# A two-block recurrent and attention model on one core: the values' product per head on its half of the array, sums through DRAM as whole rows, and eight planned times

## The chip, the cores and the metric

The kernel runs on one core of a Trainium2 chip. The metric is the device time of one execution in microseconds (us). Five engines work from queues of their own: TensorE (PE; PEld is its weight load), VectorE (DVE), ScalarE (ACT), GpSimd (POOL) and SyncE (SP), which here issues nearly all transfers. Each engine takes its instructions in the order in which the program has them, so an instruction that waits holds back all that stand behind it on the same engine.

## The reference, cut to what matters

Two blocks of two layers each, over 512 positions of width 1024. Each layer of the first block has three branches (a recurrence with a state per head, a retention, a gated unit), a gated merge of them, and a feed-forward part. The change touches the recurrence and two normalisations:

```python
def step(state, inp):                      # rwkv7_scan, per head of 64
    r_t, w_t, k_t, v_t, kk_t, a_t = inp
    sa = jnp.einsum('bhvk,bhk->bhv', state, -kk_t)
    state = (state * w_t[:, :, None, :] + sa[..., None] * (kk_t * a_t)[:, :, None, :]
             + v_t[..., None] * k_t[:, :, None, :])
    y = jnp.einsum('bhvk,bhk->bhv', state, r_t)
    return state, y
...
kk = kk / jnp.maximum(jnp.sqrt(jnp.sum(kk * kk, axis=-1, keepdims=True)), 1e-12)
y = rwkv7_scan(r, decay, k, v, kk, a)
mean = jnp.mean(y, axis=-1, keepdims=True)
var = jnp.mean(jnp.square(y - mean), axis=-1, keepdims=True)
y = (y - mean) * lax.rsqrt(var + RW_GN_EPS) * lnx_g + lnx_b
y = y + jnp.sum(r * k * r_k, axis=-1, keepdims=True) * v
...
y = y * lax.rsqrt(jnp.mean(y * y, axis=-1, keepdims=True) + EPS)     # retention, per head of 128
```

## The kernel before, in words

Activations lie with features on the 128 partitions and the 512 positions along the row. Every dense product is made of three matmuls of 128x512 (lines 170 to 172, tiles `pm`, and `pbr` in the merge) on weights that stream in by 512 KB and are split by ACT (`whi`, line 161) and DVE (`wlo`, line 162). A dense tile of the first block is 24 such matmuls; a product of the merge is 12. Two banks of TensorE's result memory serve `pm` and `pbr` in turn, so a tile can't start before the one two places ahead of it has been read out (`gate`, line 428; in the merge line 940, on DVE).

The recurrence of a layer works on four pairs of heads (f = 0 to 3) and four chunks each. `rw_pair` prepares a pair, two lanes of `rw_unit` compute the 16 units (pair and chunk), and `rw_final` chains the chunks' states, normalises the outputs `y` and multiplies by the gate. In a unit, `psy` takes for each of the two heads e one product with `uw` (line 685) and one with the values (line 686). The values `vp` stand in a tile of 128x4x64 with zeros in the two middle columns, so that each head's weights are 128 columns wide, half of them zero.

`sums` makes a sum over each head's features for every position: four small matmuls (line 202, result of 32 partitions for each quarter of the positions), a step on ACT or DVE (`fn`), a write to DRAM (`sumd`, line 207), and n reads (line 209) that spread each row over 128/n partitions again; n is 2 for the recurrence and 1 for retention. It is used 40 times: in each of the two layers four times each for `psk` (the length of kk, read by `kkr`, line 527), `psbon`, `psmean` (read at line 742), `psq` (line 755) and `psrn` of retention (line 825).

The order of TensorE's work in these layers is made by hand: `Plan` keeps a time, in which each step has a cost, and lets dense steps (`Dense`, `MORE`) fill what lies between the steps of chains. `Chain(cost, wait)` says that the thread's next step is due `wait` us later. The dense work is the projections, the other branches and then the gates (`gates1`), which run out last; behind them the merge begins. The other engines' orders come from a scheduler that follows this one. Instructions under `self.late()` are put behind the last read of a dense tile.

Of the kernel before, what the change touches and what calls it, by code (L numbers as in the profile page):

```python
# [10 lines left out]
F32 = mybir.dt.float32  # L11
# [7 lines left out]
S = 512  # L19
# [36 lines left out]
def Chain(cost, wait):  # L56
    return Step(cost, wait, chain=True)
# [49 lines left out]
class Kern:  # L107
# [90 lines left out]
    def sums(self, x, sel, n, ps, out, fn):  # L198

        nc = self.nc  # L200
        for g in range(4):
            nc.tensor.matmul(ps[32 * g:32 * g + 32, :], lhsT=sel, rhs=x[:, g * 128:(g + 1) * 128],
                             start=True, stop=True, skip_group_check=True)
        t = self.ap.tile([128, 128], F32, name="sums", tag="sums", bufs=2)
        fn(t, ps)
        d = self.dp.tile([4, 32, 128], F32, name="sumd", tag="sumd", bufs=8)
        nc.sync.dma_start(d.rearrange("g r t -> (g r) t"), t)
        for i in range(n):
            nc.sync.dma_start(out[i * 128 // n:(i + 1) * 128 // n, :].rearrange("p (g t) -> p g t", g=4),
                              d[:, i][None].to_broadcast([128 // n, 4, 128]))  # L210

# [258 lines left out]
    def rw_pair(self, l, f, r, k, vt, m, lora, half):  # L470
# [51 lines left out]
        nc.vector.scalar_tensor_tensor(r, r, v(V_RK + f), k2, op0=OP.mult, op1=OP.mult)  # L522
        yield Chain(0.4, 13.0)

# [73 lines left out]
    def lane(self, l, i):  # L598

        while self.units:  # L600
            f, g = self.units[0]
            if f > 1 and not self.ended[f - 2]:
                yield Chain(0.0, 1.0)
                continue
            self.units.pop(0)
            if g == 0:
                self.states[f] = dict((n, self.tile("WK", (128, 8, 64), name=n)) for n in ("y0", "rdw", "xt", "cc"))
            yield from self.rw_unit(f, g, self.states[f], i)
            self.left[f] -= 1
            if not self.left[f]:  # L610
                self.plan.add(self.rw_final(l, f, self.states[f]), 0, 2.0)

    def rw_unit(self, f, g, st, lane):
# [16 lines left out]
        nc.vector.tensor_copy(tk, pst[:, 1:3, :])  # L630
        vp = self.vp[lane]
        nc.scalar.activation(vp[:, 0:4:3, :], pst[:, 3, :].rearrange("p (e v) -> p e v", e=2), AF.Copy)
        rhs = small([128, 2, 128], "rhs")
# [25 lines left out]
        for e in range(2):  # L659
            nc.tensor.matmul(psv[:, e, :], lhsT=ams[e][:, 256:384], rhs=vp[:, 3 * e, :],  # L660
                             start=True, stop=True)
# [22 lines left out]
        for e in range(2):  # L684
            nc.tensor.matmul(psy[:, e, :], lhsT=uw[:, e, :], rhs=ams[e][:, 128:256], start=True, stop=False)
            nc.tensor.matmul(psy[:, e, :], lhsT=vp[:, 2 * e:2 * e + 2, :].rearrange("p a v -> p (a v)"),
                             rhs=ams[e][:, 384:512], start=False, stop=True)
        for e in range(2):
# [6 lines left out]
        for m in range(3):  # L695
            for e in range(2):
                for c in range(2):
                    cs = slice(64 * c, 64 * c + 64)
                    os = ws = slice(64 - 64 * e, 128 - 64 * e)
                    us = slice(64 * e, 64 * e + 64)  # L700
                    b_ = tk[cs, 0, us]
                    o, x, y, first, last = ((0, uw[cs, e, ws], b_, True, True), (1, b_, uw[cs, e, us], True, False),
                                            (1, tk[cs, 1, us], vp[cs, 3 * e, :], False, True))[m]
                    nc.tensor.matmul(psx[c][os, o, :], lhsT=x, rhs=y, start=first, stop=last, skip_group_check=True)
# [5 lines left out]
    def rw_final(self, l, f, st):  # L710
# [5 lines left out]
        nc.vector.tensor_tensor(cc[:, 0:7, :], cc[:, 0:7, :], d[:, 0:7].unsqueeze(2).to_broadcast([128, 7, 64]), op=OP.mult)  # L716
        yield Chain(0.0, 1.0)
        for c in range(1, 7):
# [8 lines left out]
        for c in range(1, 8):  # L727
            cs = slice(64 * c, 64 * c + 64)
            for e in range(2):
# [9 lines left out]
                  lambda t, ps: nc.scalar.activation(t, ps, AF.Copy, scale=-1.0 / 64))  # L739
        yield Chain(0.4, 10.0)  # L740
        with self.late():
# [10 lines left out]
        nc.scalar.activation(gt, psg, AF.Copy)  # L752
        yield Chain(1.6, 11.0)
        with self.late():
# [14 lines left out]
    def retention(self, l, win):  # L769
# [4 lines left out]
        for f in range(2):  # L774
# [19 lines left out]
            for e in range(2):  # L794
# [24 lines left out]
                self.norms(sq, self.sel[:, 1], 1, self.PF([128, 128], "psrn"), bias=self.eps[:, 0:1], scale=1.0 / 128)  # L819
                self.plan.add(self.ret_end(l, h, y, sq), 0, 12.0)  # L820
                yield Dense(0.4)
# [978 lines left out]
    def run(self):  # L1800
# [3 lines left out]
        with ExitStack() as ctx:  # L1804
# [11 lines left out]
            if L1:  # L1816
                g12 = self.cp.tile([128, 8], F32, name="g12")
                nc.vector.tensor_tensor(g12, V[:, 16:24], V[:, 24:32], op=OP.mult)
                with block(self, "act"):
# [13 lines left out]
                    self.am = [self.ap.tile([128, 2, 4, 128], F32, name="am%d" % i) for i in range(2)]  # L1833
                    self.vp = [self.ap.tile([128, 4, 64], F32, name="vp%d" % i) for i in range(2)]
                    for t in self.am:
                        nc.gpsimd.memset(t.rearrange("p e m t -> p (e m t)"), 0.0)
                    for t in self.vp:
                        nc.gpsimd.memset(t.rearrange("p a v -> p (a v)"), 0.0)
                    for l in range(L1):
# [303 lines left out]
```

## Time and profile before

| | |
|---|---|
| median of 3 runs | 3266.28 us (3265.93 to 3267.68) |
| profiled execution: its own time | 3264.7 us |
| profiled execution: span of the trace | 3263.0 us |
| PE busy | 3208.0 us, 98% of the span |
| DVE busy | 2187.2 us, 67% |
| ACT busy | 1362.0 us, 42% |
| mean granted clock of TensorE | 0.996 of full speed |

All times below are from the one profiled execution, counted from the start of its span. The merges of the first block's two layers begin near 487 and 1440 us. A wait is the idle time of an engine in front of an instruction, named by what ended it.

### The profile page before, as it was taken

To read this page: it belongs to the slowest core of one execution; us is meant where nothing else is said; L and a number is where in the kernel's file an instruction comes from. 1 tells how busy PE (TensorE), PEld (TensorE's weight loads), DVE (VectorE), ACT (ScalarE), POOL (GpSimd) and SP (SyncE) were. 2 spreads that over 40 slices of the span, in tenths; PEclk is the share of its full clock that TensorE was granted. 3 is DMA by queue.
4 is the path that set the end of the run, shared out by engine and by line. 5 is a ranking of instruction groups with operands and counts; after the bars stand their busy time and mean duration, and the time that the engine had idled before them with its cause. 6 is when DMAs were issued, how large, how long until landed. Compare 5 with 4: busy or idle time off the path is not lost.

```text
span 3263.0 us, 47497 instructions
## 1 busy us (share of the span) xinstructions
PE 3208.0 (98%) x17992; PEld 2574.7 (79%) x17992; DVE 2187.2 (67%) x4071; ACT 1362.0 (42%) x2442; POOL 124.9 (4%) x176
## 2 busy tenths in 40 slices
PE   8999999999999999999999999999999999999998
PEld 6787877888887787878888887877788888777777
DVE  6875656777537855656677456987666669866665
ACT  5533434444335333434444334344334443443343
POOL 0000000000000000000000000010003100100031
PEclk9999999999999999999999999999999999999999
DMA  4433245433433423245333436453355564534464
GB/s 148 132 99 88 85 137 178 127 102 97 139 107 108 130 82 96 81 156 180 101 97 98 150 122 206 143 148 109 118 194 187 175 174 139 152 109 124 151 213 145
DMA packets 199797, 434.75 MB, mean 133 GB/s; under 512 B 29833, under 2 KB 58633, under 8 KB 199569
## 3 DMA queue, kind: packets, MB, share of 16 engines
q1 hardware_dynamic: 197904, 429.62, 42.8%
q8 instruction: 142, 2.33, 0.3%
q0 software_dynamic: 512, 1.05, 0.1%
q10 hardware_dynamic: 1152, 1.05, 0.1%
q14 instruction: 87, 0.70, 0.1%
HBM read 339.05 MB, written 61.36 MB: 123 GB/s over the span
## 4 chain that ended last, share of the span: by engine, by line
PE 82%; DVE 8%; DMA 6%; issue 2%; ACT 2%; SPq 0%; POOL 0%; DVEq 0%; ACTq 0%; POOLq 0%
PE pm L170 21%; PE pm L172 21%; PE pm L171 21%; PE psy L1186 2%; PE pbr L170 2%; PE pbr L171 2%; PE pbr L172 2%; PE pspt L1176 2%; DVE wlo L162 2%; DMA rdw<-sumd 1%; DMA sqr<-sumd 1%; PE psl L1158 1%; PE psl L1159 1%; DMA sqk<-sumd 1%; DMA sumd<-sums 1%
## 5 line engine op out<-in xcount | busy, mean ns | idle before, releaser
L170 PE MATMUL pm<-shi,whi 128*128 128x512 f32 x3064 | 1227.0, 400 | 0.9 <-ACT whi L161 0.9
L172 PE MATMUL pm<-shi,wlo 128*128 128x512 f32 x3064 | 1202.2, 392 | 1.4 <-DVE wlo L162 1.4
L171 PE MATMUL pm<-slo,whi 128*128 128x512 f32 x3064 | 1201.0, 392 | 0.0
L161 ACT ACTIVATE whi<-wraw 128x1024 fp32r<-128x1024 f32 x480 | 508.4, 1059 | 887.0 <-PE pm L171 527.6
L162 DVE TENSOR_TENSOR wlo<-wraw,whi 128x1024 fp32r<-128x1024 f32 x480 | 588.1, 1225 | 198.4 <-ACT whi L161 193.1
L170 PEld LDWEIGHTS pm<-shi,whi 128*128 128x128 f32 x3064 | 577.3, 188 | 138.4 <-issue 26.9
L172 PEld LDWEIGHTS pm<-shi,wlo 128*128 128x128 f32 x3064 | 576.6, 188 | 125.8 <-DVE wlo L162 4.0
L171 PEld LDWEIGHTS pm<-slo,whi 128*128 128x128 f32 x3064 | 577.5, 188 | 111.7 <-issue 4.1
L428 DVE TENSOR_TENSOR ev<-pm,rb 128x512 f32<-128x512 f32 x138 | 94.7, 687 | 110.9 <-PE pm L172 110.1
L897 DVE TENSOR_TENSOR gate<-pm,rb 128x512 f32<-128x512 f32 x80 | 55.0, 688 | 127.3 <-PE pm L172 127.0
L170 PE MATMUL pbr<-shi,whi 128*128 128x512 f32 x288 | 113.8, 395 | 1.1 <-DVE gate L940 0.8
L170 PE MATMUL pm<-whi,shi 128*128 128x256 f32 x384 | 112.5, 293 | 1.3 <-DVE ev L428 1.3
L171 PE MATMUL pbr<-slo,whi 128*128 128x512 f32 x288 | 112.2, 390 | 0.0
L172 PE MATMUL pbr<-shi,wlo 128*128 128x512 f32 x288 | 112.2, 389 | 0.0
L171 PE MATMUL pm<-wlo,shi 128*128 128x256 f32 x384 | 108.9, 284 | 0.6 <-DVE wlo L162 0.6
L172 PE MATMUL pm<-whi,slo 128*128 128x256 f32 x384 | 108.9, 284 | 0.0
L940 DVE SCALAR_TENSOR_TENSOR gate<-gate,pbr 128x512 f32<-128x512 f32 x128 | 85.7, 683 | 29.1 <-PE pbr L172 28.5
L944 POOL TENSOR_TENSOR gate<-gate 128x512 f32<-128x512 f32 x48 | 78.0, 1626 | 590.5 <-DVE gate L940 335.6
L937 ACT ACTIVATE gate<-gate 128x512 f32<-128x512 f32 x128 | 76.2, 625 | 46.0 <-DMA gate<-gtd 40.1
L1143 ACT ACTIVATE p<-psl,st 128x256 f32<-128x256 f32 (+3 forms) x128 | 65.1, 512 | 60.4 <-DVE st L1141 50.9
L170 PEld LDWEIGHTS pm<-whi,shi 128*128 128x128 f32 x384 | 73.6, 192 | 3.8 <-DVE ev L428 1.7
L171 PEld LDWEIGHTS pm<-wlo,shi 128*128 128x128 f32 x384 | 73.8, 192 | 1.3 <-DVE wlo L162 1.1
(524 smaller groups left out, 4401.8 us busy)
## 6 DMA issues: line engine op xcount, KB each, us to landing
wraw<-in_w_gt SPq DMA_DIRECT2D x148, 512.0 KB, 3.6
wraw<-in_w_in SPq DMA_DIRECT2D x116, 512.0 KB, 3.6
wraw<-in_f_up SPq DMA_DIRECT2D x88, 512.0 KB, 3.5
gtd<-gate SPq DMA_DIRECT2D x116, 256.0 KB, 2.0
gate<-gtd SPq DMA_DIRECT2D x116, 256.0 KB, 4.2
wraw<-in_w_br SPq DMA_DIRECT2D x44, 512.0 KB, 3.7
wraw<-in_f_dn SPq DMA_DIRECT2D x44, 512.0 KB, 3.5
wraw<-in_w_out SPq DMA_DIRECT2D x32, 512.0 KB, 3.7
```

Of the source, the lines that this page charges most:

```text
L161: nc.scalar.activation(hi[:, :n], raw[:, :n], AF.Copy)
L162: nc.vector.tensor_tensor(lo[:, :n], raw[:, :n], hi[:, :n].bitcast(F32), op=OP.subtract)
L170: nc.tensor.matmul(ps, lhsT=lhs[0], rhs=rhs[0], start=first, stop=False, skip_group_check=skip)
L171: nc.tensor.matmul(ps, lhsT=lhs[0], rhs=rhs[1], start=False, stop=False, skip_group_check=skip)
L172: nc.tensor.matmul(ps, lhsT=lhs[1], rhs=rhs[0], start=False, stop=last, skip_group_check=skip)
L428: self.last = self.nc.vector.tensor_tensor(t, ps, self.rb, op=OP.mult)
L937: nc.scalar.activation(g, g, AF.Tanh, scale=0.5)
L940: nc.vector.scalar_tensor_tensor(g, g, 1.0, pb, op0=OP.add, op1=OP.mult)
L944: (nc.gpsimd if self.pre and n in self.cfg.get("pa", (1, 2, 3)) else nc.vector).tensor_tensor(g, g, acc[c], op=OP.add)
L1143: nc.scalar.activation(p[:, :w], l, AF.Exp, bias=st[:, 0:1], accum_out=st[:, 1:2])
L1176: nc.tensor.transpose(pt_[:, b * 128:(b + 1) * 128], ps[e][:, b * 128:(b + 1) * 128], self.ident)
L1186: nc.tensor.matmul(psy[64 * e:64 * e + 64, :], lhsT=vs[e][b], rhs=pts[e][:, b * 128:(b + 1) * 128], start=first and b == 0, stop=last and ...
```

## The change

In a unit, the product with the values loses its padding: `vp` becomes a tile of 128x2x64 of the unit's own, each head's weights are 64 columns, and its result goes to the head's 64 partitions alone. The order of the four products changes from uw, values, uw, values to both uw, then both values. The two padded tiles and the zeroing of them on POOL go. In `sums`, only the rows that are read later go to DRAM, n writes of four partitions instead of one of 128; a sum's 512 positions then lie in one piece, and each read fetches rows of 2 KB instead of four pieces of 512 B. Eight planned times change.

```diff
@@ sums
-        d = self.dp.tile([4, 32, 128], F32, name="sumd", tag="sumd", bufs=8)
-        nc.sync.dma_start(d.rearrange("g r t -> (g r) t"), t)
+        d = self.dp.tile([n, 4, 128], F32, name="sumd", tag="sumd%d" % n, bufs=8)
         for i in range(n):
-            nc.sync.dma_start(out[i * 128 // n:(i + 1) * 128 // n, :].rearrange("p (g t) -> p g t", g=4),
-                              d[:, i][None].to_broadcast([128 // n, 4, 128]))
+            nc.sync.dma_start(d[i], t[i:128:32, :])
+        for i in range(n):
+            nc.sync.dma_start(out[i * 128 // n:(i + 1) * 128 // n, :],
+                              d[i].rearrange("g t -> (g t)")[None].to_broadcast([128 // n, S]))
@@ rw_pair, between the sum psk and its use in kkr
-        yield Chain(0.4, 13.0)
+        yield Chain(0.4, 15.0)
@@ lane, start of rw_final; rw_final, before the chain of states
-                self.plan.add(self.rw_final(l, f, self.states[f]), 0, 2.0)
+                self.plan.add(self.rw_final(l, f, self.states[f]), 0, 2.5)
-        yield Chain(0.0, 1.0)
+        yield Chain(0.0, 2.5)
@@ rw_unit
-        vp = self.vp[lane]
-        nc.scalar.activation(vp[:, 0:4:3, :], pst[:, 3, :].rearrange("p (e v) -> p e v", e=2), AF.Copy)
+        vp = small([128, 2, 64], "vp")
+        nc.scalar.activation(vp, pst[:, 3, :].rearrange("p (e v) -> p e v", e=2), AF.Copy)
...
         for e in range(2):
-            nc.tensor.matmul(psy[:, e, :], lhsT=uw[:, e, :], rhs=ams[e][:, 128:256], start=True, stop=False)
-            nc.tensor.matmul(psy[:, e, :], lhsT=vp[:, 2 * e:2 * e + 2, :].rearrange("p a v -> p (a v)"),
-                             rhs=ams[e][:, 384:512], start=False, stop=True)
+            nc.tensor.matmul(psy[:, e, :], lhsT=uw[:, e, :], rhs=ams[e][:, 128:256], start=e == 0, stop=False,
+                             skip_group_check=True)
+        for e in range(2):
+            nc.tensor.matmul(psy[64 * e:64 * e + 64, e, :], lhsT=vp[:, e, :], rhs=ams[e][:, 384:512], start=False,
+                             stop=True, skip_group_check=True)
@@ rw_final, from psmean to its use, and from psq to its use
-        yield Chain(0.4, 10.0)
+        yield Chain(0.4, 7.5)
-        yield Chain(1.6, 11.0)
+        yield Chain(1.6, 8.5)
@@ retention, from psrn to its use
-                self.plan.add(self.ret_end(l, h, y, sq), 0, 12.0)
+                self.plan.add(self.ret_end(l, h, y, sq), 0, 9.0)
@@ run
-                    self.vp = [self.ap.tile([128, 4, 64], F32, name="vp%d" % i) for i in range(2)]
-                    for t in self.vp:
-                        nc.gpsimd.memset(t.rearrange("p a v -> p (a v)"), 0.0)
```

What this does to the orders is shown at three places. The first is TensorE in a unit of the recurrence, before:

```order
L678 MATMUL psu<-rhs,tt 128x128 x2
L685 MATMUL psy<-am_235,uw 128x128
L686 MATMUL psy<-am_235,vp_237 128x128
L685 MATMUL psy<-am_235,uw 128x128
L686 MATMUL psy<-am_235,vp_237 128x128
L704 MATMUL psx<-tk,uw 64x64 x4
```

And the same unit in the changed program:

```order
L680 MATMUL psu<-rhs,tt 128x128 x2
L687 MATMUL psy<-am_235,uw 128x128 x2
L690 MATMUL psy<-am_235,vp 64x128 x2
L708 MATMUL psx<-tk,uw 64x64 x4
L708 MATMUL psx<-uw,tk 64x64 x4
```

The two products with the values stand together, have 64 result partitions each, and stand directly ahead of the 64x64 products.

The second place is DVE around the beginning of the merge in layer 0, where `y_3695` is the output of the last pair (f = 3), line 216 the last step of its sum `psq`, line 755 its first use, and line 940 reads out a product of the merge. Before:

```order
L216 RECIPROCAL sums<-sums 128x128
L940 SCALAR_TENSOR_TENSOR gate<-gate,pbr 128x512 x2
L944 TENSOR_TENSOR gate<-gate 128x512
L162 TENSOR_TENSOR wlo<-wraw,whi 128x1024
L755 TENSOR_TENSOR y_3695<-y_3695,rdw 128x512
L940 SCALAR_TENSOR_TENSOR gate<-gate,pbr 128x512
L756 TENSOR_SCALAR y_3695<-y_3695,vec_243 128x512
```

The same place in the changed program (lines 218, 759 and 944 are those called 216, 755 and 940 above; `y_3680` is the same output):

```order
L218 RECIPROCAL sums<-sums 128x128
L430 TENSOR_TENSOR gate<-pm,rb 128x512
L162 TENSOR_TENSOR wlo<-wraw,whi 128x1024
L759 TENSOR_TENSOR y_3680<-y_3680,rdw 128x512
L944 SCALAR_TENSOR_TENSOR gate<-gate,pbr 128x512
L760 TENSOR_SCALAR y_3680<-y_3680,vec_239 128x512
L761 TENSOR_TENSOR y_3680<-y_3680,xt 128x512
L762 TENSOR_TENSOR y_3680<-cc,y_3680 128x512
L944 SCALAR_TENSOR_TENSOR gate<-gate,pbr 128x512
```

One more dense tile is read out between the sum and its use, and the use stands ahead of the merge's first read-out instead of its third. On TensorE, the four matmuls of `psq` and the one of `psgate` now stand ahead of the last 24 dense matmuls; before, the merge's first product followed on them at once. Layer 1 has the same two orders at its merge.

The third place is SP's queue there, before (line 907 stores a gate, line 934 loads one):

```order
L157 DMA wraw<-in_w_br 128x1024
L207 DMA sumd<-sums 128x128
L209 DMA rdw<-sumd 64x4x128 x2
L934 DMA gate<-gtd 128x512
L157 DMA wraw<-in_w_br 128x1024
```

And in the changed program:

```order
L157 DMA wraw<-in_w_br 128x1024
L209 DMA sumd<-sums 4x128 x2
L211 DMA rdw<-sumd 64x512 x2
L911 DMA gtd<-gate 128x512
L157 DMA wraw<-in_w_br 128x1024 x2
L938 DMA gate<-gtd 128x512 x2
```

Two small writes stand for one, and the reads have rows of 512 elements. In `rw_pair`, 60 dense matmuls stand between the matmuls of `psk` and of `psbon` (which is where `kkr` is due) for every pair in the changed program; before it was 60 for the first pair and 54 for the other three. From `psbon` on to `psA` it stays 24 for the first three pairs and becomes 30 for the fourth. (A matmul of 256 columns is counted as half of one.)

## Rows read from the trace of the kernel before

**Rows 1.** The page, busy time of TensorE and its granted clock in 40 slices.
```profile
PE 3208.0 (98%) x17992; PEld 2574.7 (79%) x17992; DVE 2187.2 (67%) x4071; ACT 1362.0 (42%) x2442; POOL 124.9 (4%) x176
PEclk9999999999999999999999999999999999999999
```

**Rows 2.** The waits of TensorE: us in total, times, longest.
```profile
PE pbr L170 <- DVE gate L940: 6.6, 4, 2.9
PE psA L546 <- DVE kkr L533: 5.6, 5, 1.8
PE psam L651 <- ACT rhs L635: 3.6, 4, 1.2
PE psu L678 <- DVE rhs L674: 1.8, 2, 1.5
```

**Rows 3.** Timeline at layer 0's merge: start, us, engine, line, [idle before].
```profile
485.82 0.43 PE L202 MATMUL psq<-rdw,sel 128*32 128x128 f32 x8
...
492.10 1.24 SPq L209 DMA_DIRECT2D rdw<-sumd  x2
...
497.61 0.39 PE L171 MATMUL pbr<-slo,whi 128*128 128x512 f32 x1
497.83 0.39 PE L172 MATMUL pbr<-shi,wlo 128*128 128x512 f32 x1
499.69 0.69 DVE L755 TENSOR_TENSOR y<-y,rdw 128x512 f32<-128x512 f32 x1 [4.33 <-DMA rdw<-sumd]
501.13 0.63 PE L170 MATMUL pbr<-shl,whi 128*128 128x512 f32 x1 [2.91 <-DVE gate L940]
```

**Rows 4.** Stretches: PE busy (instructions), PEld, DVE, ACT, POOL, granted clock, DMA share.
```profile
74.00:77.00 3.00, 2.32 (x38) 2.03 (x39) 3.00 (x5) 1.81 (x5) 0.00 (x0) 1.00 0.22 60
501.00:504.00 3.00, 2.87 (x7) 2.33 (x8) 2.90 (x5) 2.71 (x4) 0.00 (x0) 0.55 0.00 0
1027.00:1030.00 3.00, 3.00 (x8) 2.31 (x8) 2.93 (x7) 2.91 (x8) 0.00 (x0) 0.50 0.46 95
```

**Rows 5.** Timeline at layer 1's merge, TensorE.
```profile
1453.55 0.71 PE L170 MATMUL pbr<-shl,whi 128*128 128x512 f32 x1 [2.89 <-DVE gate L940]
```

**Rows 6.** Timeline of kkr on DVE and psA on TensorE, first pairs of both layers.
```profile
68.36 0.75 DVE L527 SCALAR_TENSOR_TENSOR kkr<-mix,vec,sqk 128x512 f32<-128x512 f32 x1 [1.07 <-DMA sqk<-sumd]
...
74.68 0.98 PE L546 MATMUL psA<-kr,kkr 64*64 64x64 f32 x32 [1.50 <-DVE kkr L533]
...
1019.26 0.75 DVE L527 SCALAR_TENSOR_TENSOR kkr<-mix,vec,sqk 128x512 f32<-128x512 f32 x1 [1.35 <-DMA sqk<-sumd]
...
1025.59 0.97 PE L546 MATMUL psA<-kr,kkr 64*64 64x64 f32 x32 [1.79 <-DVE kkr L533]
```

**Rows 7.** DMA issues: count, KB each, median us from issue to landing.
```profile
hi<-hi SPq DMA_DIRECT2D x68, 128.0 KB, 2.6
...
sumd<-sums SPq DMA_DIRECT2D x40, 64.0 KB, 1.8
...
sqr<-sumd SPq DMA_DIRECT2D x8, 256.0 KB, 8.3
...
rdw<-sumd SPq DMA_DIRECT2D x16, 128.0 KB, 5.7
...
cumb<-cumd SPq DMA_DIRECT2D x8, 256.0 KB, 3.7
```

**Rows 8.** Timeline of TensorE in a unit, and a pair of half-array products in block 2.
```profile
203.95 0.39 PE L685 MATMUL psy<-am,uw 128*128 128x128 f32 x2
...
204.40 0.39 PE L685 MATMUL psy<-am,uw 128*128 128x128 f32 x2
...
204.94 0.35 PE L704 MATMUL psx<-tk,uw 64*64 64x64 f32 x8
...
2785.03 0.44 PE L1186 MATMUL psy<-pt,vf 128*64 128x128 f32 x4
...
2785.40 0.50 PE L171 MATMUL pm<-slo,whi 128*128 128x512 f32 x1
```

More of the change, by code (lines that the diff above doesn't have):

```diff
@@ L659, in rw_unit @@
         for e in range(2):
-            nc.tensor.matmul(psv[:, e, :], lhsT=ams[e][:, 256:384], rhs=vp[:, 3 * e, :],
+            nc.tensor.matmul(psv[:, e, :], lhsT=ams[e][:, 256:384], rhs=vp[:, e, :],
                              start=True, stop=True)
@@ L702, in rw_unit @@
                     o, x, y, first, last = ((0, uw[cs, e, ws], b_, True, True), (1, b_, uw[cs, e, us], True, False),
-                                            (1, tk[cs, 1, us], vp[cs, 3 * e, :], False, True))[m]
+                                            (1, tk[cs, 1, us], vp[cs, e, :], False, True))[m]
                     nc.tensor.matmul(psx[c][os, o, :], lhsT=x, rhs=y, start=first, stop=last, skip_group_check=True)
```

## The prediction, before the changed kernel had run

> **What bounds the kernel now.** The page comes first. TensorE is busy for 98% of the span [rows 1], so a transfer or a step of another engine counts only where TensorE stands still for it, or slows down. The list of TensorE's waits tells where: in the first block, 6.6 us at `pbr` for the read-out on line 940 and 5.6 us at `psA` for `kkr`; next come 3.6 us at `psam` and 1.8 us at `psu`, which wait for small steps of the lanes [rows 2]. The first two are this change's subject, since both go back to `sums`.
>
> The timeline at layer 0's merge shows how. `psq` runs at 485.82; its spreading reads are issued at 492.10; DVE stands 4.33 us for them and starts line 755 at 499.69. Behind it on DVE waits the read-out of the merge's third product (line 940), and for that bank waits the merge's fifth product: the last matmul before it starts at 497.83, the next at 501.13 [rows 3]. Matmuls of this size follow each other every 0.23 us (497.61 to 497.83), so the hole is 3.30 - 0.23 = 3.07 us. Then the clock is down: 0.55 granted from 501 to 504, with 7 matmuls in 3 us instead of 13 [rows 4]. Seven at 0.23 are 1.6 us of work, so 1.4 us are lost, with the ends 1.5. Layer 1 shows the same hole: 2.89 us of idle time before the product of the same name, 2.91 in layer 0 [rows 3, 5].
>
> At `psA` the same kind of thing is smaller. In the first pair of each layer DVE starts `kkr` 1.07 and 1.35 us late because its sum has not come back, and `psA` starts 1.50 and 1.79 us late [rows 6]. After the second of these the clock is at 0.50, with 8 matmuls in 3 us: another 1.2 us, with the ends 1.4. After the first it stayed at 1.00 [rows 4].
>
> **A, the product with the values.** Today the four products of a unit and the step to `psx` take 204.94 - 203.95 = 0.99 us; two products alone take 204.40 - 203.95 = 0.45 [rows 8]. What remains of the 0.99 is the other two, 0.45, and 0.09 for going over to 64x64 products. After the change the two with `uw` cost 0.45. Then comes one more change of form, 0.09. The two half-wide ones have a direct counterpart in block 2, two heads' products of 128x64 weights on both halves: four passes and the change back to another form take 2785.40 - 2785.03 = 0.37 [rows 8]. Sum 0.91, 0.08 less, times 32 units: **-2.6 us**. At worst the halves don't run beside each other, and four passes take 0.45 as now with the extra change of 0.09 on top: +2.9 us. The Trainium skill's TensorEngine Tiling (Array Packing), section Tiling Modes, says that a change of mode drains TensorE, while tiles of one mode work in parallel. The first half speaks against this edit and the trace bears it out with the 0.09 at `psx`; the second half is what the 0.37 shows. By the first alone the term would be the +2.9.
>
> **B, the merges.** Two things move. The planner sets `psq` 24 dense matmuls (5.45 us) ahead of the merge, but DVE's order puts line 755's instruction ahead of the first read-out instead of the third. Two products of the merge are 24 matmuls as well, so the place at which TensorE must stop for it is as far from `psq` as now: 12.24 us (485.82 to 498.06). The earlier `psq` therefore gains nothing by itself, and what counts is how much sooner the sum comes back: it needs 3.07 us.
>
> From the first read's issue to DVE's start it now takes 7.6 us [rows 3]. A read of 128 KB whose rows are long lands in 2.6 us (`hi`), a spread of one 2 KB row over 128 partitions, 256 KB, in 3.7 (`cumb`); the same 256 KB in pieces of 512 B takes 8.3 (`sqr`) [rows 7]. `cumb` has the form of the new reads. Two reads of 128 KB, the second issued up to 0.6 us after the first (1.24 us for both in rows 3), should take 3.2 to 4.3: 3.3 to 4.4 less. The write (1.8 us for 64 KB, rows 7) becomes two writes of 2 KB; the second adds up to 0.6, and I count 0.3. So 3.0 to 4.1 of the 3.07 needed come: a hole of 0.2 may stay, and the clock stays up, as it did after 1.50 us in rows 4. **2 x (3.07 - 0.2 + 1.5) = -8.7 us**. If the reads get no faster, it is 0.
>
> The Trainium skill's DMA: Bandwidth & Descriptors, section Specifications, gives 512 B as the least transfer for full rate. By that the pieces of 512 B are already good enough and B would be 0. The trace disagrees: 8.3 against 3.7 us for the same bytes.
>
> **C, psA.** `kkr` is due 2 us later in the plan, which is one group of 6 matmuls (1.36 us) for three pairs of each layer and nothing for the first, and its sum comes some 3 us sooner. DVE's standing for it goes. What remains of `psA`'s waits is DVE's own work after `kkr`: 1.50 - 1.07 and 1.79 - 1.35 in the first pairs, and small change in the others, 1.1 us together by my count. So 5.6 - 1.1 = 4.5, and the slow stretch after 1025.59, 1.4: **-5.9 us**, with 0 as the other end, if DVE's later place for `kkr` makes `psA` as late as before.
>
> **What costs nothing.** DVE also stands for the sums at lines 742, 755 and 825 in the middle of the layers, where the plan is cut by 2.5 to 3 us. The transfers shorten by about as much, so it should stand as long as now. Its cover is the dense tile of 24 matmuls, 5.45 us, with a second bank behind it; where that cover has failed so far, TensorE lost 1.8 us (`psu`, rows 2). SP issues 32 more writes, but its queue is paced by DVE and the reads take less to issue. The removed zeroing on POOL lies ahead of the first units, off any chain: POOL works 4% of the span [rows 1]. The rest of the reshuffling moves lane steps by a few groups; the waits that it can remove or double are those of `psam` and `psu`, 3.6 and 1.8 us [rows 2]. I take 0, with 5 either way.
>
> **Sum.** -2.6 - 8.7 - 5.9 = -17.2. The profiled execution took 3264.7, so 3247.5; the median of the runs lies 1.6 above it: **3249 us**.
>
> **Rivals.**
> *The hole at the merge stays, because the reads are no faster.* Their time would be set by the weights' 512 KB loads that share the queue, and by the one row that all partitions fetch. For it: those issued at 492.10 took 7.6 against a median of 5.7 for their group [rows 3, 7]. Against it: `sqr` against `cumb`. B falls away, and of C half: 3249 + 8.7 + 3 = 3261. 12%. This is also the time that the Trainium skill's 512 B (DMA: Bandwidth & Descriptors, Specifications) would give.
> *Half-way.* The reads gain 2 us instead of 3.5: holes of 1.2 us at both merges with the clock still falling in one of them, `psA` half cured. 3249 + 2.0 + 1.5 + 3 = 3256. 20%.
> *The halves don't overlap.* A becomes +2.9 with the rest as forecast: 3254. 8%.
> *Slower: the sum comes back later than now.* The n writes go from four partitions each, one behind the other, ahead of the reads, and the queue's order makes every read wait for them. The Trainium skill's DMA: Bandwidth & Descriptors, section Why a DMA increments its semaphore by 16 and not by 1, has such a write on four engines instead of sixteen; no run here has shown one. If the writes take 3 us more and the reads gain nothing, the merges' holes grow by 3 each (+6), and `psA` waits longer by 3 us less the 1.36 of the plan in six pairs and 3 in two, at most +16. With A that gives 3269 to 3286, around 3278. From 1.5 us of net delay on, the kernel is slower than before. 7%.
>
> **How the numbers follow.** The forecast itself, 3244 to 3253, has 53%. With the halves' case and the half-way case it is 81%, all faster than 3259.7, which is 0.2% below the median (0.2%, 6.5 us, is about what a measurement of this kernel can tell). Of the 12% at 3261, a third falls on the faster side by A's and C's ends. So faster 0.84, but the plan's other moves may cost what I put at 0, and I take off 0.06: **faster 0.78, same 0.15, slower 0.07**. The range has to reach the half-way case and the upper rival's foot: **3243 to 3262**, leaving out the slow case and what lies over it.
>
> **What would show it.** In the profile after: at the merges, no gap above 0.5 us in front of the fifth product, and a granted clock of 1.00 behind it; the reads of `sums` at 2.6 to 3.7 us; `psA` waiting 1 to 2 us in all; `psy` to `psx` 0.91 us in a unit. The prediction is wrong if the reads still take over 5 us, if a new row above 3 us stands among TensorE's waits in the first block, or if the slow stretches stay three.

## The result, and the profile after

The changed kernel takes **3232.31 us** (median; 3231.39 to 3235.24) against 3266.98 (3265.93 to 3273.31) for the kernel before, run beside it: a ratio of 0.9891, 95% interval 0.9874 to 0.9909. That is faster, as forecast, but by 34.7 us instead of the 17.2 of the sum, and it lies 11 us under the foot of the range. The profiled execution took 3232.33 us, with a span of 3230.6. (The title and the section on the change speak of eight planned times; the diff shows that there are six.)

The page, TensorE's line (compare [rows 1]) and the shares of the chain that ended last:

```profile
PE 3196.7 (99%) x17992; PEld 2560.1 (79%) x17992; DVE 2185.8 (68%) x4071; ACT 1362.5 (42%) x2442; POOL 124.9 (4%) x174
...
PE 92%; DVE 4%; DMA 1%; ACT 1%; issue 1%; SPq 0%; POOL 0%; DVEq 0%; ACTq 0%; POOLq 0%
```

TensorE's busy time is 11 us shorter for almost the same work (the slow stretches of before are part of that), and the other 21 us were gaps. The same chain of before:

```profile
PE 82%; DVE 8%; DMA 6%; issue 2%; ACT 2%; SPq 0%; POOL 0%; DVEq 0%; ACTq 0%; POOLq 0%
```

Transfers made up 6% of it and now make up 1%. TensorE's waits (compare [rows 2]; engine, line, what ended the wait, us in total, times, longest):

```profile
PE pbr L170 <- DVE gate L944: 1.9, 3, 1.2
PE psA L548 <- DVE kkr L535: 1.6, 4, 0.5
```

`pbr` fell from 6.6 to 1.9 us and `psA` from 5.6 to 1.6. (Of the 6.6, which the prediction puts in the first block, 5.8 lie at the two merges [rows 3, 5] and 0.8 in block 2; the 1.9 lie in block 2 alone.) But `psam` (3.6 before) and `psu` (1.8) are not in the list at all, which goes down to 0.2 us, and these two the prediction had counted with 0. Nor are other small steps of the first block that stood in the list of before and not among [rows 2], of which the largest are:

```profile
PE psret L812 <- DVE pret L810: 2.3, 3, 1.0
...
PE psz L722 <- DVE am L656: 1.0, 2, 0.5
```

With four rows of 0.2 to 0.6 us (`psz`, `psx` twice, `pst`) the waits of TensorE for such steps came to 10.5 us before. None of them is in the list after.

Layer 0's merge (compare [rows 3]; start, us, engine, line, [idle before]):

```profile
469.20 0.42 PE L202 MATMUL psq<-rdw,sel 128*32 128x128 f32 x8
...
472.88 1.10 SPq L209 DMA_DIRECT2D sumd<-sums  x2
...
474.83 1.12 SPq L211 DMA_DIRECT2D rdw<-sumd  x2
...
476.00 0.39 PE L170 MATMUL pbr<-shi,whi 128*128 128x512 f32 x1
...
478.34 0.69 DVE L759 TENSOR_TENSOR y<-y,rdw 128x512 f32<-128x512 f32 x1
...
479.40 0.39 PE L170 MATMUL pbr<-shi,whi 128*128 128x512 f32 x1
```

From the first read's issue to DVE's use it is 478.34 - 474.83 = 3.5 us, where it was 7.6. From the first write's issue to the first read's it is 1.95, where it was 2.60 (489.50 to 492.10 [rows 3]):

```profile
489.50 0.32 SPq L207 DMA_DIRECT2D sumd<-sums  x1
```

TensorE has no gap here. In layer 1 DVE waits 0.69 us for the same sum, 3.9 us after the first read's issue, and TensorE not at all:

```profile
1409.51 1.12 SPq L211 DMA_DIRECT2D rdw<-sumd  x2
...
1413.37 0.69 DVE L759 TENSOR_TENSOR y<-y,rdw 128x512 f32<-128x512 f32 x1 [0.69 <-DMA rdw<-sumd]
```

Behind both merges the clock stays up, with 15 matmuls in 3 us (compare [rows 4]: 7 at a granted clock of 0.55); the third row is a slow stretch in block 2, of which more below:

```profile
478.00:481.00 3.00, 3.00 (x15) 2.45 (x15) 2.88 (x6) 0.00 (x0) 0.00 (x0) 1.00 0.69 196
...
1414.00:1417.00 3.00, 3.00 (x15) 2.48 (x14) 2.93 (x6) 1.20 (x2) 0.00 (x0) 1.00 0.41 162
...
1970.00:1973.00 3.00, 3.00 (x16) 2.34 (x15) 2.37 (x7) 1.60 (x4) 0.00 (x0) 0.50 0.86 264
```

A unit's products (compare [rows 8]): from `psy` to `psx` it is 204.30 - 203.39 = 0.91 us, the 0.91 of the forecast.

```profile
203.39 0.60 PE L687 MATMUL psy<-am,uw 128*128 128x128 f32 x4
203.93 0.44 PE L690 MATMUL psy<-am,vp 128*64 128x128 f32 x4
204.30 0.34 PE L708 MATMUL psx<-tk,uw 64*64 64x64 f32 x8
```

So the signs that the prediction asked for are there, as far as the trace shows them: the landings of the reads by themselves are not recorded in it, only the 3.5 and 3.9 us from issue to use of two reads. What it had not asked for is who else waited for the sums. In the kernel before, DVE stood 50.2 us for them (us, times):

```profile
  DVE y L755: 19.9, 6
  DVE yret L825: 12.2, 4
  DVE y L742: 9.8, 4
  DVE kkr L527: 8.3, 6
```

How such a standing reaches TensorE shows in layer 1 of the kernel before. DVE stands 6.42 us for retention's sum; the small step `rhs` of a lane is next in its queue, and TensorE's `psu` stands 1.53 us for that step:

```profile
1285.53 0.69 DVE L825 TENSOR_TENSOR yret<-yret,sqr 128x512 f32<-128x512 f32 x1 [6.42 <-DMA sqr<-sumd]
1286.14 0.42 DVE L674 TENSOR_TENSOR rhs<-psh,rhs 128x256 f32<-128x256 f32 x1
...
1286.61 0.71 PE L678 MATMUL psu<-rhs,tt 128*128 128x128 f32 x4 [1.53 <-DVE rhs L674]
```

After the change DVE stands 16.0 us:

```profile
  DVE yret L829: 14.4, 4
  DVE y L759: 1.2, 2
  DVE y L746: 0.4, 1
```

**Where the 32 us lie.** TensorE's work of the first block falls into three stretches per layer: up to the last matmul of `psA` (the preparation), from there to the first of `pbr` (the units, with the dense tiles), and the matmuls of `pbr` (the merge). Their lengths are the differences of those matmuls' starts in each trace, in us; the column in the middle also holds the feed-forward part of layer 0, and the last one, from the last `pbr` of layer 1 to TensorE's last matmul, that of layer 1. Kernels named here are the experiments below.

| kernel | prep. 0 | units 0 | merge 0 | to last psA of layer 1 | units 1 | merge 1 | block 2 |
|---|---|---|---|---|---|---|---|
| before | 134.9 | 351.9 | 70.3 | 529.6 | 352.6 | 70.3 | 1746.9 |
| after | 134.7 | 341.3 | 65.1 | 528.0 | 341.3 | 65.1 | 1748.6 |
| e1: new transfers alone | 132.0 | 346.4 | 65.8 | 525.0 | 346.3 | 65.6 | 1747.5 |
| e7: all but the planned times | 131.8 | 345.9 | 65.7 | 525.4 | 345.9 | 65.6 | 1750.5 |
| e2: planned times alone | 136.2 | 374.7 | 67.6 | 530.1 | 374.3 | 71.4 | 1750.9 |
| e11: transfers of psk, last psq | 131.9 | 358.6 | 65.8 | 525.4 | 356.2 | 65.8 | 1751.3 |
| e12: transfers of the others | 136.3 | 347.0 | 71.5 | 526.6 | 346.4 | 70.4 | 1751.1 |

With the new planned times 12 dense matmuls per layer (12 x 0.227 = 2.7 us) stand in the preparation and no longer among the units. Set right for that, the change brought 5.2 + 5.2 at the merges, 2.9 + 4.3 in the preparation, and 7.8 + 8.6 = 16.4 among the units, where 2.6 were forecast. Block 2, which the change doesn't touch, took 1.7 longer: a slow stretch there (granted 0.50, above) is 6.8 us long instead of 3.4.

### The profile page after: what moved, and what is told of

Its sections match the earlier page's. It is cut to its first block, busy times and chain, and to the rows that moved or that the text cites. A ratio compares the mean times of both kernels' runs of the same rounds, so it can differ in the third digit from the quotient of the medians.

```text
span 3230.6 us, 47555 instructions
## 1 busy us (share of the span) xinstructions
PE 3196.7 (99%) x17992; PEld 2560.1 (79%) x17992; DVE 2185.8 (68%) x4071; ACT 1362.5 (42%) x2442; POOL 124.9 (4%) x174
## 4 chain that ended last, share of the span: by engine, by line
PE 92%; DVE 4%; DMA 1%; ACT 1%; issue 1%; SPq 0%; POOL 0%; DVEq 0%; ACTq 0%; POOLq 0%
PE pm L170 24%; PE pm L172 23%; PE pm L171 23%; PE pbr L170 2%; PE psy L1190 2%; PE pbr L171 2%; PE pbr L172 2%; PE pspt L1180 2%; DVE wlo L162 1%; PE psl L1162 1%; PE psl L1163 1%; PE pssc L811 1%; PE psam L653 1%; PE psret L816 1%; DMA zd<-z 1%
## 5 line engine op out<-in xcount | busy, mean ns | idle before, releaser
L1147 ACT ACTIVATE p<-psl,st 128x256 f32<-128x256 f32 (+3 forms) x128 | 65.1, 512 | 60.4 <-DVE st L1145 51.0
```

The source lines that it names most:

```text
L1147: nc.scalar.activation(p[:, :w], l, AF.Exp, bias=st[:, 0:1], accum_out=st[:, 1:2])
```

## The experiments

Ratios are to the kernel before, run on the same chip; its medians there were 3271.33 us (e1 to e4), 3267.95 (e5 to e8) and 3267.95 (e9 to e12). "TensorE's order is that of ..." means that its instructions stand in the same order.

**e1, the transfers alone.** The kernel before with the new `sums` and nothing else.

```diff
-        d = self.dp.tile([4, 32, 128], F32, name="sumd", tag="sumd", bufs=8)
-        nc.sync.dma_start(d.rearrange("g r t -> (g r) t"), t)
+        d = self.dp.tile([n, 4, 128], F32, name="sumd", tag="sumd%d" % n, bufs=8)
...
+            nc.sync.dma_start(d[i], t[i:128:32, :])
...
+                              d[i].rearrange("g t -> (g t)")[None].to_broadcast([128 // n, S]))
```

> The kernel before with the new form of the sums' transfers alone; planned times and the product with the values as before. Theory T (transfers): DVE's standing for the sums at lines 742, 755 and 825 held up small lane steps behind it, so the unforecast 14 us come from shorter reads; this kernel then gains 20 to 28 us, to 3239 to 3247, and DVE's waits for sums fall from 50 us to under 10. Theory P (plan): the 14 us come from where the planned times put the lanes' steps; this kernel then gains only the merges and part of psA, 10 to 15 us, to 3252 to 3257, with the waits at psam and psret as before.

Measured: 3238.60 us (3236.95 to 3239.09), ratio 0.9899 (0.9884 to 0.9914). TensorE's order is that of before. DVE's standing for the sums is all but gone (us, times):

```profile
  DVE y L757: 0.4, 1
  DVE yret L827: 0.4, 1
```

The transfers bring nearly the whole gain. By the table it lies in three places: merges -9.1, preparation -7.5, units -11.7. The last was forecast as nothing. Among the units, TensorE's waits for small steps fall from 10.5 to 1.3 us (`psz` 0.6, `psx` 0.4, `psam` 0.3), which is most of it.

**e2, the planned times alone.** The kernel before with the six planned times.

```diff
...
-        yield Chain(0.4, 10.0)
+        yield Chain(0.4, 7.5)
-        yield Chain(1.6, 11.0)
+        yield Chain(1.6, 8.5)
...
-                self.plan.add(self.ret_end(l, h, y, sq), 0, 12.0)
+                self.plan.add(self.ret_end(l, h, y, sq), 0, 9.0)
```

> The kernel before with the changed planned times alone. Theory T: the shorter planned times with the old transfers let DVE stand 2.5 to 3 us longer at each use of a mean, a variance and a retention sum; the time stays or grows, 3263 to 3280. Theory P: 10 to 16 us are gained, to 3251 to 3257, since the lane steps move as in the changed kernel.

Measured: 3315.78 us (3313.67 to 3322.19), ratio 1.0137 (1.0122 to 1.0153): 45 us slower, more than either theory allowed. Who waits for the sums:

```profile
  DVE yret L825: 48.9, 8
  DVE y L755: 29.6, 8
  DVE y L742: 5.5, 5
```

And TensorE's waits, which are again for small steps of DVE and ACT:

```profile
PE psam L651 <- ACT rhs L635: 10.2, 6, 3.2
PE pst L625 <- ACT cc L707: 8.9, 2, 4.5
PE pbr L170 <- DVE gate L940: 8.7, 5, 3.7
```

DVE's standing in mid-layer is thus not covered: the units' stretches are 23 and 22 us longer, though the 12 matmuls have left them.

**e3, the values alone.** The kernel before with the half-array product and the unit's own `vp`.

```diff
...
-            nc.tensor.matmul(psy[:, e, :], lhsT=vp[:, 2 * e:2 * e + 2, :].rearrange("p a v -> p (a v)"),
-                             rhs=ams[e][:, 384:512], start=False, stop=True)
+            nc.tensor.matmul(psy[64 * e:64 * e + 64, e, :], lhsT=vp[:, e, :], rhs=ams[e][:, 384:512], start=False,
+                             stop=True, skip_group_check=True)
```

> The kernel before with the product with the values on half of the array, and its own tile for the values, alone. Theories T and P: 2 to 3 us less, 3263 to 3265, a unit's psy to psx at 0.91 us. Theory V (values): the tile of the unit's own instead of one fixed per lane lets the next unit's first steps go ahead, and psam's waits vanish here too; 6 to 9 us less, 3258 to 3261.

Measured: 3269.83 us (3265.11 to 3274.44, 11 runs), ratio 0.9997 (0.9988 to 1.0006). The interval, -4 to +2 us, holds both the 2.6 us that were forecast and nothing, so the run can't tell them apart. Theory V falls: `psam` waits 4.0 us, where it was 3.6. What has grown is a wait for ACT behind `psy`, 0.6 us in the kernel before:

```profile
PE psx L706 <- ACT cc L709: 3.1, 4, 1.0
```

**e4 and e5, how far the pieces lie from each other.** The changed kernel, but a row of 512 positions lies in DRAM as four pieces of 512 B again, 1 KB apart (e4) or 16 KB apart (e5). The orders on TensorE and DVE are those of the changed kernel in both.

```diff
-        d = self.dp.tile([n, 4, 128], F32, name="sumd", tag="sumd%d" % n, bufs=8)
+        d = self.dp.tile([n, 4, 256], F32, name="sumd", tag="sumd%d" % n, bufs=8)
...
-                              d[i].rearrange("g t -> (g t)")[None].to_broadcast([128 // n, S]))
+                              d[i][:, 0:128][None].to_broadcast([128 // n, 4, 128]))
```

(256 for e4, 4096 in its place for e5.)

> The changed kernel, but the sum's row lies in DRAM in four pieces with gaps, so that each read again fetches 512 B at a time; the writes keep their new form. If the length of the rows is what shortens the reads, the hole at the merges and the waits at psA come back and DVE stands some 3 us at most sums: 3255 to 3275. If the gain of the transfers came from the writes (2 KB instead of 64 KB), this kernel is within 5 us of the changed one, 3232 to 3237.

> The changed kernel, but the four pieces of a sum's row lie 16 KB apart in DRAM, as they did before the change; writes small as in the changed kernel, orders of TensorE and DVE the same as there. Spacing theory: reading the same four far pieces 64 or 128 times is what made the spreads slow; DVE's waits for sums come back as in the run with the planned times alone (85 us there) and the time is 3280 to 3320. Write theory: the slow part was reading behind a write of 64 KB from 128 partitions; then this kernel stays at 3232 to 3238.

Measured: e4 3234.74 us (3232.40 to 3235.81), ratio 0.9885 (0.9872 to 0.9899); e5 3326.68 us (3322.32 to 3331.91), ratio 1.0178 (1.0160 to 1.0196). Who waits for the sums in e4:

```profile
  DVE yret L829: 15.3, 4
  DVE y L759: 2.9, 5
```

And in e5:

```profile
  DVE yret L829: 46.5, 8
  DVE y L759: 23.3, 8
  DVE y L746: 19.4, 6
  DVE kkr L529: 11.4, 4
```

The same number of pieces, of the same length, in the same order of work: 92 us lie between 1 KB and 16 KB of spacing (96 by the two ratios), and e5 lies 7 us over the spacing theory's range. The length of the pieces is worth nothing measurable: e4's interval overlaps with that of the changed kernel.

**e6, a large write.** The changed kernel with pieces 1 KB apart and all 128 partitions written, in four writes of 32.

```diff
-        d = self.dp.tile([n, 4, 128], F32, name="sumd", tag="sumd%d" % n, bufs=8)
+        d = self.dp.tile([32, 4, 256], F32, name="sumd", tag="sumd", bufs=8)
+        for g in range(4):
+            nc.sync.dma_start(d[:, g, 0:128], t[32 * g:32 * g + 32, :])
...
```

> The changed kernel, but all 128 partitions of a sum go to DRAM again, 64 KB in four writes of 32 partitions; the pieces that are read lie 1 KB apart. Write theory: 3280 to 3320, as with the planned times alone. Spacing theory: 3233 to 3245, a little above the changed kernel for two or three more writes on the queue at each sum.

Measured: 3235.77 us (3234.00 to 3238.56), ratio 0.9900 (0.9885 to 0.9915). The interval overlaps with that of the changed kernel: that 64 KB are written, and not 2 or 4, makes no difference that could be told here. Its trace also has the landings of reads of pieces 1 KB apart, where `sqr` took 8.3 us and `rdw` 5.7 with 16 KB [rows 7] (count, KB each, median us from issue to landing):

```profile
sqr<-sumd SPq DMA_DIRECT2D x8, 256.0 KB, 3.4
...
rdw<-sumd SPq DMA_DIRECT2D x16, 128.0 KB, 3.0
```

**e7, the changed kernel with the old planned times.** The edit of e2 the other way round, on the changed kernel.

```diff
...
-        yield Chain(0.4, 7.5)
+        yield Chain(0.4, 10.0)
...
-        yield Chain(1.6, 8.5)
+        yield Chain(1.6, 11.0)
...
```

> The changed kernel with the six planned times of before: transfers and values alone. If the planned times give what the changed kernel has over the transfers alone (3238.6 there), this is 3236 to 3239; if the product with the values gives it, 3231 to 3234.

Measured: 3238.21 us (3235.35 to 3239.22), ratio 0.9905 (0.9891 to 0.9920), about 6 us over the changed kernel by the medians and 5 by the ratios, whose intervals overlap, so the times alone don't settle it. The stretches of the table give the planned times a small gain with fast reads, 5 us; in e2, with slow ones, they cost 45 us. Among the units, TensorE waits in e7 for a step that is neither in e1's list nor in that of the changed kernel:

```profile
PE psx L708 <- ACT cc L711: 1.9, 2, 0.9
```

**e8, retention's planned time alone back.** DVE's standing of 14.4 us at line 829 is the largest that is left.

```diff
-                self.plan.add(self.ret_end(l, h, y, sq), 0, 9.0)
+                self.plan.add(self.ret_end(l, h, y, sq), 0, 12.0)
```

> The changed kernel with retention's use of its sum due 12 us after it, as before, instead of 9. DVE stands 14 us at that use in the changed kernel. If this standing still costs TensorE time, 1 to 4 us less, 3228 to 3231; if the dense tile covers it, no difference beyond 1 us.

Measured: 3232.85 us (3231.50 to 3235.63), ratio 0.9891 (0.9873 to 0.9908): no difference. DVE's standing there is halved:

```profile
  DVE yret L829: 6.9, 2
```

The time doesn't move with it, and the units' stretches are 341.3 us in both layers, as in the changed kernel. So this standing is covered, as the prediction took all of it to be.

**e9 and e10, which spacing is slow.** e9 is the kernel before with four more rows in the DRAM tile, so that the pieces lie 18 KB apart and not 16; its orders on TensorE and DVE are those of before.

```diff
-        d = self.dp.tile([4, 32, 128], F32, name="sumd", tag="sumd", bufs=8)
-        nc.sync.dma_start(d.rearrange("g r t -> (g r) t"), t)
+        d = self.dp.tile([4, 36, 128], F32, name="sumd", tag="sumd", bufs=8)
+        nc.sync.dma_start(d[:, 0:32], t)
```

> The kernel before, with one difference: the DRAM tile of a sum has 36 rows in place of 32 for each quarter of the positions, so the four pieces of 512 B that a read takes lie 18 KB apart in place of 16 KB. Orders on TensorE and VectorE are those of before. Theory 'any far spacing is slow': the reads stay slow, 3262 to 3275 us, no difference from before. Theory 'the power of two is slow' (pieces 16 KB apart fall on the same place in DRAM, 18 KB apart they don't): the reads are as fast as pieces near each other, 3235 to 3242 us, as with the new transfers alone.

e10 is e4 with 4 KB between the pieces:

```diff
-        d = self.dp.tile([n, 4, 256], F32, name="sumd", tag="sumd%d" % n, bufs=8)
+        d = self.dp.tile([n, 4, 1024], F32, name="sumd", tag="sumd%d" % n, bufs=8)
```

> The changed kernel with the four pieces of a row laid 4 KB apart in DRAM (1 KB apart gave 3234.7 us, 16 KB apart 3326.7). If the cost comes with a certain power of two at or under 4 KB, as slow as with 16 KB: above 3300 us. If it grows with the spacing: 3245 to 3290. If 4 KB is still near: 3231 to 3238 us.

Measured: e9 3243.31 us (3240.40 to 3244.41), ratio 0.9923 (0.9910 to 0.9935); e10 3247.23 us (3245.84 to 3249.79), ratio 0.9938 (0.9926 to 0.9951). e9 lies 1 us over the range of its second theory, e10 in the middle one of its three. In e9's trace the landings are shown (count, KB each, median us from issue to landing):

```profile
sqk<-sumd SPq DMA_DIRECT2D x32, 128.0 KB, 3.1
...
cc<-sumd SPq DMA_DIRECT2D x16, 128.0 KB, 3.1
rdw<-sumd SPq DMA_DIRECT2D x16, 128.0 KB, 3.1
```

For the same reads, of the same pieces, behind the same weights on the same queue, the kernel before has:

```profile
sqk<-sumd SPq DMA_DIRECT2D x32, 128.0 KB, 5.5
...
cc<-sumd SPq DMA_DIRECT2D x16, 128.0 KB, 4.9
```

(`rdw` had 5.7 [rows 7].) 2 KB more of spacing bring 25 us, where all of the new transfers brought 33 (e1, both by their ratios). So it isn't distance that is slow: 18 KB is fast and 16 KB is not. (The padding also moves the eight buffers of the DRAM tile from 64 to 72 KB apart. In e6 they lie 128 KB apart, and its reads are fast.) Pieces 4 KB apart lie between: DVE stands 40.8 us for the sums in e10 (23.9 at line 829, 11.5 at 759, 5.4 at 746), 18.2 in e4.

**e11 and e12, the counted sums and the others.** The kernel before with the new transfers for a part of the 40 sums: in e11 for `psk` and for the last pair's `psq`, whose gain the prediction counted; in e12 for all but these. TensorE's order is that of before in both.

```diff
-    def sums(self, x, sel, n, ps, out, fn):
+    def sums(self, x, sel, n, ps, out, fn, near=False):
...
+        if near:
+            d = self.dp.tile([n, 4, 128], F32, name="sumd", tag="sumd%d" % n, bufs=8)
...
-        self.norms(sq, self.sel[:, 0], 2, self.P([128, 128], "psq"), bias=self.eps[:, 1:2], scale=1.0 / 64)
+        self.norms(sq, self.sel[:, 0], 2, self.P([128, 128], "psq"), f == 3, bias=self.eps[:, 1:2], scale=1.0 / 64)
```

> The kernel before with the new transfers for ten of its 40 sums only: psk (read by kkr, ahead of psA) of every pair and psq of the last pair of each layer (at the merge): those whose gain the prediction counted, 8.7 us at the merges and at most 5.9 at psA. The other sums keep the old transfers; TensorE's order is that of before. All 40 with new transfers gained 28 us. If the prediction's 'what costs nothing' is right, VectorE's standing for the other sums is covered and these ten bring all of it: 3238 to 3243 us. If that standing costs TensorE time, these bring about half: 3250 to 3257 us.

> The complement: the kernel before with the new transfers for the other 30 sums (psmean, psbon, retention's psrn, and psq of the first three pairs), and the old ones for psk and the psq at the merges. TensorE's order is that of before. If VectorE's standing for these sums in mid-layer is covered, as the prediction counted: no difference from before, 3264 to 3270 us. If it costs what the spans of the changed kernel's trace left unexplained: 3250 to 3257 us, and the two halves' gains add up to the 28 us of all.

Measured: e11 3260.61 us (3255.97 to 3263.97, 10 runs), ratio 0.9976 (0.9966 to 0.9985); e12 3255.79 us (3253.03 to 3259.07), ratio 0.9963 (0.9950 to 0.9975). The sums that were counted bring 7 us by themselves, those put at nothing 12; together they brought 28 to 38 in e1 (its interval), so each half brings more where the other is there. e11 came out between its two ranges and e12 within the second, but the two gains don't add up to that of all.

The table says how. In e12 the units' stretches are 4.8 and 6.2 us shorter, as in e1 (5.5 and 6.2): these 11 us belong to the sums in mid-layer. In e11 the merges are 4.4 shorter each and the preparations 3.0 and 4.2, as in e1, but the units' stretches are 6.7 and 3.7 *longer*. There the reads for `psmean`, still slow, are awaited longer than before, DVE (9.8 us in 4 became)

```profile
  DVE y L751: 14.0, 3
```

and the next step on TensorE waits with it, which it didn't in the kernel before:

```profile
PE psq L202 <- ACT rdw L753: 4.0, 2, 2.7
```

with a slow stretch behind it (granted 0.54, 4 matmuls in 3 us), one of three among the units (the others granted 0.67 from 211 to 214 and 0.56 from 297 to 300), where the kernel before has none:

```profile
1246.00:1249.00 3.00, 2.98 (x4) 0.82 (x4) 2.52 (x4) 1.85 (x3) 0.63 (x1) 0.54 0.31 124
```

The clock stands at half for 17 us in these three stretches, so by estimate some 8.5 of the 10.4 us are its part. This execution took 3263.3 us, near the slowest of the ten, so others lost less. Why the wait for `psmean` is longer there, no run has settled.

## Why the prediction was wrong in size

**The direction and the places were right, and one term was mis-sized: "What costs nothing".** It was 0, with 5 either way, and it measured -15.4: 16.4 us of gain among the units, less about 1.0 for A (13.8, if all of A's 2.6 is there, see below). e1 and e12 give 11.7 and 11.0 of it to the reads in mid-layer, and the difference of e7 and the changed kernel gives 3.7 to the planned times (4.6 + 4.6 less the 2 x 2.7 of moved matmuls). The step that failed is "the transfers shorten by about as much [as the plan is cut], so it should stand as long as now", with the cover of "the dense tile of 24 matmuls" behind it. The transfers shortened by more than the plan was cut: DVE's standing fell from 50.2 to 16.0 us, and to 0.8 with the old planned times (e1). The cover failed where a lane's small step stood behind DVE's standing, as in the rows on `psu` above; what is left, retention's 14.4, costs nothing that could be measured (e8). The view that could have told is the list of waits itself: `psam` 3.6 and `psu` 1.8 [rows 2] wait for small steps of the lanes that stand in DVE's and ACT's queues, and DVE's standing is ahead of some of these. They were read as waits of their own, where a cover had failed here and there, and were given 5 either way, not as the far end of DVE's waits for the sums. The list was also read short: the prediction went from `psam` to `psu` and left out `psret`, 2.3, which stands between them, and five smaller ones, 10.5 us in all instead of 5.4. With the new transfers 1.3 is left of them (e1), with the new planned times nothing.

**B, the merges: forecast -8.7, measured -10.4** (5.22 + 5.20; 9.1 by the transfers alone in e1). (The 13 matmuls that the prediction gives 3 us at full clock follow from their pace; the view that has 7 of them in the slow stretch counts 15 at full clock.) The holes are gone altogether, with the slow stretches behind them. The time of the reads was right, 3.5 and 3.9 us from the first issue to DVE's use where 3.2 to 4.3 were expected. **Its reason was wrong.** `sqr` with 8.3 us against `cumb` with 3.7 was read as short pieces against a long row. But `sqr`'s pieces also lay 16 KB apart, and this is what counts: pieces of the same length 1 KB apart (e4, and `sqr` with 3.4 us in e6) or 18 KB apart (e9) are as fast or nearly so, and with 16 KB (e5) the changed kernel is slow too. The prediction said that the trace disagrees with the 512 B of the Trainium skill's DMA: Bandwidth & Descriptors, section Specifications. It doesn't: by e4 pieces of 512 B are good enough, as the page has it. The same page, in its section Latency and other measured facts, tells of copies that run slower at row pitches of 2, 4 and 8 MiB, hardly so at 512 KiB, and that get their full rate back at 4 MiB by 4 KiB of padding. The runs agree in kind, with padding of 2 KB (e9), but show the effect at 16 KB, where the page has nothing; whether the cause is the same no run shows.

**C, psA: forecast -5.9, measured -7.2** (2.9 + 4.3 in the preparation, with all that else lies there; 7.5 in e1). DVE no longer stands for `kkr`, and the new due time didn't make `psA` late. The forecast had tied the gain to both the due time and the reads; e1 shows that the reads are enough.

**A, the values: forecast -2.6, measured -1.0.** In a unit the 0.91 us came out as worked out. In the stretches e7 is only 0.5 us per layer shorter than e1 among the units, and e3 measures no difference. Where the other 1.6 went, the traces tell: among the units of both layers TensorE is busy for 691.37 us in e1 and 688.93 in e7, 2.4 less, nearly the forecast, but it stands 1.9 us at `psx` for a step of ACT that didn't hold it up in e1. In e3 the same wait has grown from 0.6 to 3.1. So the work was saved, and a wait has taken most of it. In the changed kernel, with the new planned times, this wait is gone, so there A may be worth its 2.6.

**The planned times.** They were costed at C and otherwise at nothing. Alone they cost 45 us (e2); with the fast reads they gain 5 us by the stretches, the end of the wait at `psx` among them. A wait in the plan is only as good as the transfer under it.

**The rivals.** None of the four came. The slower one feared the small writes of four partitions. At the merge the reads are issued 1.95 us after the first write, where it was 2.60 after the one large write, so no delay is seen. That such a write runs on four engines (the Trainium skill's DMA: Bandwidth & Descriptors, section Why a DMA increments its semaphore by 16 and not by 1) no run here shows. (The chance of "faster" adds up to 0.85 before the deduction, where the prediction has 0.84; nothing hangs on it.)

## What to carry to other kernels

Where one engine's queue stands for a transfer, list everything that stands behind it and who waits for that, and sum it over the whole kernel before calling it covered: here the standing in mid-layer was worth more than the holes that were easy to see. When two transfers of the same size take different times, change one thing at a time before naming the cause; length and spacing of the pieces differed together. And a small row that many partitions read again should not lie in pieces 16 KB apart: near each other (1 KB, e6) or with four rows of padding (18 KB, e9) a read of 128 KB took 3.0 to 4.0 us instead of 4.9 to 5.7. A power of two alone isn't slow, since 1 KB is one.

## What the runs showed of the hardware that was not expected

Reads that spread four pieces of 512 B over 64 partitions take a median of 4.9 to 5.7 us when the pieces lie 16 KB apart, and 3.1 when they lie 18 KB apart. With 1 KB they take 3.0 to 4.0 (e6), and the kernel is as fast as with one piece of 2 KB (e4); with 4 KB it is 12 us slower by the medians, 17 by the ratios (e10 against e4). Which part of the memory is behind this the runs don't show.

In block 2, whose instructions are the same in both kernels, the slow stretch that lasts 3.4 us in the execution of before (from 2003.1) lasts 6.8 us in that of after (from 1968.5). Block 2 differs by up to 4 us between the kernels of the table, so a difference of 1 or 2 us in one execution says little.
